# A hybrid encoder layer: a new beginning, and the squares of queries and keys folded onto 64 partitions

## The chip, the cores and the metric

The kernel is one program on one core of one Trainium2 chip. The metric is the device time of an execution in microseconds (us). Three executions of the kernel before took 1318.42, 1318.89 and 1319.12 us. One more was taken with the profiler, and all rows quoted here come from that one. A core has five engines with queues of their own: PE (TensorE, the matmuls), ACT (ScalarE), DVE (VectorE), POOL (GpSimd) and SP (which here only issues DMAs). An instruction waits in the queue of its engine until the semaphores that it names have been reached, and everything behind it on that engine waits with it.

## The reference, cut to what matters

One layer on a sequence of 512 frames with 2048 channels, all in float32:

```python
hn = rmsnorm(x, norm_g)
proj = hn @ w_in                      # q, k, v, gate path of three branches, 4 forget logits, 3 x 2048 merge gates
qa, ka = rmsnorm(q_A, g0), rmsnorm(k_A, g1)      # per head, over its 128 channels
ya = softmax(qa ka^T * scale + c_q - c_k) v_A    # forgetting attention, causal
qb, kb = rmsnorm(q_B, g2), rmsnorm(k_B, g3)
yb = softmax(qb kb^T * scale + rel_bias) v_B     # banded by chunks of 64
yc = stick_breaking(q_C, k_C, v_C)               # no norm of q and k
ys = [ya, yb, yc] * silu(gate path)
merged = sum(sigmoid(gates) * (ys @ w_up))
out = x + merged @ w_out
```

Each branch has 4 heads of 128 channels. So the norm of a query or a key, one sum of 128 squares per frame, is taken 16 times: 4 heads, branches A and B, query and key.

## The kernel before, in words

Everything is transposed: a tile has 128 channels on the partitions and the 512 frames along its rows. A float32 matmul is done with two float32r parts of each operand: the high part is the rounded value, the low part is what is left. `split` makes them, the high part with an ACT copy (L245), the low part with a DVE subtraction (L249). Three products, high by high, high by low and low by high, make one full product.

The kernel is a list of *units*, blocks of weights that are loaded (SP, and POOL where a second block is added in the DMA), split into `wh` and `wl`, and used by the matmuls of L264. The first quad of units computes q, k, v and gate path of the head C0 directly, while x is still arriving. The units after it take pairs of columns with Strassen's seven products, with sums of blocks made on DVE (L631, L637). Attention of the heads is put between the units: C0 to C3, B0 to B3, A0 to A3. Then come the up projections, the merge and the output projection.

The order of work on PE, ACT and DVE is not written out by hand. A planner (`Flow`, L62) runs over generators at build time. Each `yield` names an engine and an estimated cost, or an event or a free buffer to wait for; the planner takes at each step the piece that can start first, and issues it. What comes out is a fixed order on each engine. If a cost in a generator is changed, then pieces around it can change places. POOL and SP are ordered by the program's own order.

The beginning (L291 to L334). `begin_in` is one tile with 128 x 645 floats: the first 512 columns are the channels 0 to 127 of x, and the other 133 are the constants `norm_g` (16), `qk_norm_g` (4), `b_f` (1), `b_gate` (48) and the weights of the forget logits (64). It is SP's first DMA (L294). The first block of weights is ACT's first DMA. POOL sets constants; `onef`, the ones, is its third tile. DVE copies `gqk` into `gq` (L328), scales two columns of it (L330), and copies the forget weights into `w2` (L333), as soon as `begin_in` is there. PE has 16 matmuls of the ones with themselves (L1553, 128x256, bfloat16), whose result nobody reads. Then `prep_x(0)` makes the high part of the first x tile on DVE (L433), `prep` the high part of the first weights on ACT in two halves (L388), and the first matmul of L264 takes both.

The norm of a query or key is `Head.normed`: a multiplication with the norm of x (DVE, L513); the squares (ACT, L912); `split` of the squares (ACT L245 into `sqh`, DVE L249 into `sql`); two matmuls with a matrix of ones that add up over the partitions (L919 for `sqh`, L920 for `sql`, into one PSUM tile); then `rsqrt` with ACT's logarithm and exponential and a step of Newton (L455 to L467); the product with `gq` (L928), and the split into `qkh` and `qkl` that the scores use (L259 to L261). `t2s` counts free tiles of 128x512 floats, `atts` the PSUM tiles for attention.

Of the kernel before, what the change touches and what calls it, by code (L numbers as in the profile page):

```python
# [8 lines left out]
F32 = mybir.dt.float32  # L9
F32R = mybir.dt.float32r  # L10
BF16 = mybir.dt.bfloat16
AF = mybir.ActivationFunctionType
ALU = mybir.AluOpType
AX = mybir.AxisListType

P = 128
S = 512
D = 2048
HD = 128
NH = 4  # L20
W = 512
NB = 3
KT = D // P
QB = S // P
DT = D // P
UK = 8
NQ = 4
HS = S // 2
EPS = 1e-6
NEG = -1e30  # L30
SCALE = HD ** -0.5
# [4 lines left out]
PE, ACT, DVE = 0, 1, 2  # L36
# [26 lines left out]
class Flow:  # L63
# [16 lines left out]
    def give(self, slots, n=1):  # L80
        slots.free += [self.fin] * n

    def spawn(self, gen, slack, ready=None):
        task = Task(gen, slack, self.now if ready is None else ready)
        self.tasks.append(task)
        self.advance(task)
# [62 lines left out]
def mm_us(n, x=1):  # L149
    return x * max(0.115, n / 2400 + 0.0133)  # L150


def act_us(n, x=1):
    return x * (0.075 + 0.00095 * n)


def dve_us(n, x=1):
    return x * (0.1 + 0.00105 * n)
# [3 lines left out]
def hybrid_kernel(  # L162
# [2 lines left out]
    xT: bass.AP,  # L165
    xn: bass.AP,
    begin: bass.AP,
    w_one: bass.AP,
    w_two: bass.AP,
    w_col: bass.AP,  # L170
# [5 lines left out]
    nc = tc.nc  # L176
    PS = bass.MemoryType.PSUM

    cp = ctx.enter_context(tc.tile_pool(name="cp", bufs=1))
# [10 lines left out]
    def nm(s):  # L190
        uid[0] += 1
        return f"{s}_{uid[0]}"

    flow = Flow()
    spawn, set_, give = flow.spawn, flow.set, flow.give
    t2s, atts, raws, xps = Slots(NT, KEPT), Slots(4), Slots(NR), Slots(NX)
    accs = [Slots(2), Slots(1), Slots(1)]

    def t2(s, dt=F32):
        return tp.tile([P, S], dt, tag="t2", name=nm(s))  # L200

    def small(s):
        return sp.tile([P, 1], F32, tag="small", name=nm(s))

    def acc(i=0):

        return pa.tile([P, S], F32, tag=f"acc{i}", name=nm("acc"), bufs=1 if i else 2)

    def att():
        return pt.tile([P, S], F32, tag="att", name=nm("att"))  # L210

    def f(ap):
        return ap.bitcast(F32)

    def blk(i):
        return slice(i * P, (i + 1) * P)

    LH, RH = slice(0, HS), slice(HS, S)

    def two(ap):  # L220

        return ap.rearrange("p (h s) -> p h s", h=2)
# [16 lines left out]
    def pair_of(name, dt=F32R):  # L239
        return t2(name + "h", dt), t2(name + "l", dt)  # L240

    def split(hi, lo, src, n, ev=None, due=(), hi_ev=None):

        yield (ACT, act_us(n), *due)
        nc.scalar.activation(hi, src, AF.Copy)  # L245
        if hi_ev is not None:
            set_(hi_ev)
        yield (DVE, dve_us(n), *due)
        nc.vector.tensor_sub(lo, src, f(hi))  # L249
        if ev is not None:  # L250
            set_(ev)
# [38 lines left out]

    nc.scalar.preload_act_table_set("natural_log_exp_and_others")  # L291
    begin_in = cp.tile([P, begin.shape[1]], F32, name="begin_in")
    x_begin, small_in = begin_in[:, :S], begin_in[:, S:]
    first = [tc.keep_in_program_order(nc.sync.dma_start(begin_in, begin))]  # L294
    gn = small_in[:, 0:KT]
    gqk = small_in[:, KT:KT + 4]
    bfc = small_in[:, KT + 4:KT + 5]
    bg = small_in[:, KT + 5:KT + 5 + NB * DT]
    wf = small_in[:, KT + 5 + NB * DT:].rearrange("p (k h) -> p k h", h=NH)

    epsc = cp.tile([P, 1], F32, name="epsc")
    nc.gpsimd.memset(epsc, EPS)
    nhepsc = cp.tile([P, 1], F32, name="nhepsc")
    nc.gpsimd.memset(nhepsc, -0.5 * EPS)
    tmpc = t2("tmpc")
    onef, zerof, nu_f = tmpc[:, blk(0)], tmpc[:, blk(1)], tmpc[:, blk(2)]
    nc.gpsimd.memset(onef, 1.0)
    nc.gpsimd.memset(zerof, 0.0)
    ones_r = cp.tile([P, P], F32R, name="ones_r")
    nc.vector.tensor_copy(ones_r, onef)  # L310
# [14 lines left out]
    nc.gpsimd.memset(zeroc, 0.0)  # L325

    gq = cp.tile([P, 4], F32, name="gq")
    nc.vector.tensor_copy(gq, gqk)  # L328
    for c in (0, 2):
        nc.vector.tensor_scalar_mul(gq[:, c:c + 1], gqk[:, c:c + 1], SCALE)  # L330

    w2 = cp.tile([P, KT * NH + 32], F32, name="w2")
    nc.vector.tensor_copy(w2[:, :KT * NH].rearrange("p (k h) -> p k h", k=KT), wf)  # L333
    nc.vector.tensor_copy(w2[:, KT * NH:], zerof[:, :32])  # L334
    t2s.free.pop()


# [28 lines left out]
    def raw_tile(shape=(UK, P)):  # L366
        return wp.tile([P] + list(shape), F32, tag="raw", name=nm("raw"), bufs=NR)

    def load_unit(u):
        if isinstance(u, Pair):  # L370
            if u is u.task.units[0]:
                yield from u.task.load()
            return
        for s in u.srcs:
            yield raws, 1
            t = raw_tile(u.shape)
            u.raw = t
            u.there.t = fetch(t, s, flow.ready, 4 * u.shape[0] * P * P // 1024, nc.scalar if u is units[0] else nc.sync).t
# [47 lines left out]
    def prep_x(kt):  # L426

        due = (2.5 + 2.7 * place[kt],)
        yield x_in[kt]
        x, g, h, lo = xraw[kt], gn[:, kt:kt + 1], xs[kt].hi, xs[kt].lo  # L430
        if kt == 0:
            yield (DVE, 0.5, *due)
            nc.vector.tensor_scalar_mul(h, two(x), g)  # L433
        else:
            yield (ACT, act_us(S), *due)
            nc.scalar.activation(h, two(x), AF.Copy, scale=g)
        set_(raw_hi[kt])
        yield (DVE, dve_us(S), *due)
        nc.vector.scalar_tensor_tensor(lo, two(x), g, f(h), op0=ALU.mult, op1=ALU.subtract)
        set_(raw_ev[kt])  # L440

        due = (DUE[0] - 16.0 + place[kt],)
        if kt % 2 == 0:
            yield (DVE, 0.5, *due)
            nc.vector.tensor_scalar_mul(x, x, g)
        else:
            yield (ACT, 0.65, *due)
            nc.scalar.activation(x, x, AF.Copy, scale=g)
        set_(gained[kt])
# [431 lines left out]
    class Head:  # L881
# [23 lines left out]
        def normed(self, r):  # L905
            yield self.event(r)
            c = self.c[r]
            yield from by_norm(c)
            yield t2s, 3
            yield ACT, act_us(S)  # L910
            sq = t2("sq")
            nc.scalar.activation(sq, c, AF.Square)  # L912
            hi, lo = pair_of("sq")
            yield from split(hi, lo, sq, S)
            give(t2s)
            yield atts, 1
            yield PE, mm_us(S, 2)
            ps = att()
            nc.tensor.matmul(ps, ones_r, hi, start=True, stop=False)  # L919
            nc.tensor.matmul(ps, ones_r, lo, start=False, stop=True)  # L920
            give(t2s, 2)
            yield t2s, 4
            rs = t2("rs")
            yield from rsqrt(rs, ps, HD, (t2("rt"), t2("rw"), t2("rv")), S, lambda: give(atts))
            give(t2s, 3)
            i = 2 * self.n + r
            yield DVE, dve_us(S)
            nc.vector.scalar_tensor_tensor(rs, rs, gq[:, i:i + 1], c, op0=ALU.mult, op1=ALU.mult)  # L928
            give(t2s)
            yield t2s, 2  # L930
            self.c[r] = pair_of("qk")
            yield from split(*self.c[r], rs, S, self.event("p", r))
            give(t2s)
# [566 lines left out]
    def loads():  # L1500
        def x(kt):
            if kt == 0:
                xraw[kt], x_in[kt].t = x_begin, landing(0.0, 256)
                return
            yield t2s, 1
            xraw[kt] = t2("x")
            x_in[kt].t = fetch(xraw[kt], xT[kt], 0.0, 256).t

        def n(i):
            yield t2s, 1  # L1510
            t = t2("xn")
            n_in[i].t = fetch(t, xn[i // NQ, i % NQ], 0.0, 256).t
            spawn(square_x(i, t), 10.0)

        todo = list(range(NQ * QB))
        for i, sp in enumerate(spans):

            for kt in [kt for sp in spans[i:i + (2 if i > 2 else 1)] for kt in range(*sp)]:
                if xraw[kt] is None:
                    yield from x(kt)  # L1520
            yield from load_unit(units[i])
            if i >= N_FROM:
                for _ in range(N_PER):
                    if todo:
                        yield from n(todo.pop(0))
        for i in todo:
            yield from n(i)
        for u in units[len(spans):]:
            yield from load_unit(u)
# [21 lines left out]
    warm = onef.bitcast(BF16)  # L1551
    for _ in range(WARM):
        nc.tensor.matmul(first_ps[:, :2 * P], warm[:, :P], warm, start=True, stop=True)  # L1553

    line[:] = 0.8, 1.9
    flow.fin = 3.5
    spawn(loads(), 0.0, 0.0)
    for kt in range(KT):
        spawn(prep_x(kt), 5.0)
    for k in range(UK):  # L1560
        spawn(combos(k), 5.0)
    spawn(stream(), 1e9)
# [4 lines left out]
NT = 20  # L1567
KEPT = 1
AHEAD = 0.4
WARM = 16  # L1570
SPANS = [(0, 1), (1, 2)] + [(k + h, k + h + 2) for k in range(0, UK, 2) for h in (0, UK)][1:]
N_ONE = 2
NX = 28
# [56 lines left out]
```

## Time and profile before

| What | us |
|---|---|
| median of three runs (lowest, highest) | 1318.89 (1318.42, 1319.12) |
| the profiled execution's own time | 1318.54 |
| span of its instructions | 1316.8 |
| busy: PE, DVE, ACT, POOL | 1311.3, 1140.6, 807.2, 95.0 |
| instructions: PE matmuls, DVE, ACT | 7474, 1707, 1280 |
| first matmul of the warm-up, first of L264 | 1.13, 5.31 |

The span runs from the first to the last instruction of the program in the trace; 1.7 us of the execution lie around it. A row of the timeline gives the start, the time from the first start to the last end, the engine and line, what is written and read, and how many instructions were merged into the row; the bracket at the end tells the idle time before it and what ended it. A matmul's duration (0.39 us for 128x512) is longer than the distance to the next one, since matmuls are pipelined; PEld is the load of its weights. The granted TensorE clock of the execution is 1.00 throughout.

### The profile page before, as it was taken

The numbers are of one execution on the slowest core, as the hardware profiler recorded it, in microseconds if no ns is written. First come the engines' busy times: TensorE is split into PE (matmuls) and PEld (weight loads), VectorE is DVE, ScalarE is ACT, GpSimd is POOL, SyncE is SP. The second block draws the span as 40 slices with busy tenths as digits, with TensorE's granted clock in tenths as the row PEclk, the third lists the DMA queues.
The fourth block names the chain that finished last, engine by engine and source line by source line (L and its number), as shares of the span: only waits on it lengthen the run. The fifth ranks groups of instructions, "written<-read, shape, count | busy, mean of one in ns | idle before, by whom it ended". The sixth has DMA issues, their size and how long they took to land.

```text
span 1316.8 us, 20264 instructions
## 1 busy us (share of the span) xinstructions
PE 1311.3 (100%) x7474; PEld 1149.1 (87%) x7474; DVE 1140.6 (87%) x1707; ACT 807.2 (61%) x1280; POOL 95.0 (7%) x120
## 2 busy tenths in 40 slices
PE   9999999999999999999999999999999999999998
PEld 6898888888888888888888888888888888898887
DVE  8999989788898889888898989889899988897786
ACT  8766757575557665666656664666657655454443
POOL 0010100000010100101000000001000000000100
PEclk9999999999999999999999999999999999999999
DMA  9777767767776776766767767776769765668883
GB/s 339 213 204 198 183 192 185 200 186 192 201 199 187 188 200 179 219 181 189 202 179 216 188 184 199 205 185 185 195 179 280 248 219 168 206 172 253 242 248 100
DMA packets 89651, 266.24 MB, mean 202 GB/s; under 512 B 10560, under 2 KB 12608, under 8 KB 89552
## 3 DMA queue, kind: packets, MB, share of 16 engines
q1 hardware_dynamic: 70400, 203.86, 45.5%
q0 software_dynamic: 15552, 56.63, 25.4%
q10 hardware_dynamic: 3600, 4.46, 0.9%
q8 instruction: 59, 0.97, 0.3%
q14 instruction: 40, 0.33, 0.1%
HBM read 245.21 MB, written 19.70 MB: 201 GB/s over the span
## 4 chain that ended last, share of the span: by engine, by line
PE 99%; DVE 1%; DMA 0%; ACT 0%; issue 0%; ACTq 0%
PE acc L264 85%; PE att L264 8%; PE att L1022 1%; PE att L260 1%; PE att L1136 1%; PE att L261 1%; PE att L1137 1%; PE att L259 1%; PE att L1135 1%; PE att L1087 0%; PE att L1237 0%; PE att L919 0%; PE att L920 0%; DMA begin_in<-in_begin 0%; DVE m L249 0%; DVE wl L249 0%
## 5 line engine op out<-in xcount | busy, mean ns | idle before, releaser
L249 DVE TENSOR_TENSOR wl<-raw,wh 128x1024 fp32r<-128x1024 f32 (+2 forms) x418 | 499.0, 1198 | 122.2 <-ACT wh L245 121.5
L245 ACT ACTIVATE wh<-raw 128x1024 fp32r<-128x1024 f32 (+2 forms) x418 | 433.7, 1039 | 162.9 <-PE acc L264 89.9
L264 PE MATMUL acc<-x,wh 128*128 128x512 f32 (+1 forms) x1568 | 396.7, 388 | 0.7 <-DVE gq L330 0.7
L264 PEld LDWEIGHTS acc<-x,wh 128*128 128x128 f32 x1568 | 283.7, 188 | 56.1 <-issue 2.2
L264 PE MATMUL acc<-t,wh 128*128 128x512 f32 (+1 forms) x1128 | 280.3, 388 | 0.0
L264 PEld LDWEIGHTS acc<-t,wh 128*128 128x128 f32 x1128 | 200.4, 189 | 34.8
L264 PEld LDWEIGHTS acc<-x,wl 128*128 128x128 f32 x1504 | 205.9, 190 | 16.5 <-issue 0.8
L264 PE MATMUL acc<-x,wl 128*128 128x256 f32 (+1 forms) x1504 | 216.5, 285 | 0.0
L264 PE MATMUL acc<-t,wl 128*128 128x256 f32 x1104 | 156.5, 283 | 0.0
L264 PEld LDWEIGHTS acc<-t,wl 128*128 128x128 f32 x1104 | 144.7, 191 | 2.1
L282 POOL DMA_DIRECT2D raw<-in_w_col x92 | 79.7, 866 | 916.3 <-DMA raw<-in_w_col 449.3
L264 PE MATMUL acc<-m,wh 128*128 128x512 f32 (+1 forms) x512 | 109.7, 364 | 0.3 <-DVE m L249 0.3
L264 PEld LDWEIGHTS acc<-m,wh 128*128 128x128 f32 x512 | 86.3, 189 | 13.9 <-DVE m L249 0.5
L825 ACT ACTIVATE c<-acc 128x256 f32<-128x256 f32 x51 | 19.6, 384 | 90.8 <-PE acc L264 85.3
L771 ACT ACTIVATE u<-acc 128x512 f32<-128x512 f32 x52 | 31.1, 598 | 65.6 <-PE acc L264 60.3
L631 DVE TENSOR_TENSOR raw<-raw,raw 128x1024 f32<-128x1024 f32 x54 | 65.8, 1219 | 0.3
L637 DVE TENSOR_TENSOR raw<-raw,raw 128x1024 f32<-128x1024 f32 x54 | 65.8, 1218 | 0.3
L264 PE MATMUL att<-y,wh 128*128 128x512 f32 x256 | 65.8, 389 | 0.0
L792 ACT ACTIVATE u<-acc 128x512 f32<-128x512 f32 x51 | 30.3, 595 | 55.1 <-PE acc L264 54.2
L264 PEld LDWEIGHTS acc<-m,wl 128*128 128x128 f32 x448 | 58.3, 191 | 2.4
L264 PE MATMUL acc<-m,wl 128*128 128x256 f32 x448 | 59.8, 283 | 0.0
L264 PEld LDWEIGHTS att<-y,wh 128*128 128x128 f32 x256 | 48.0, 188 | 10.0
(202 smaller groups left out, 1388.6 us busy)
## 6 DMA issues: line engine op xcount, KB each, us to landing
raw<-in_w_col SPq DMA_DIRECT2D x230, 512.0 KB, 4.4
raw<-in_w_col POOLq DMA_DIRECT2D x92, 512.0 KB, 6.4
raw<-in_w_out SPq DMA_DIRECT2D x40, 512.0 KB, 4.3
gl<-c SPq DMA_DIRECT2D x48, 256.0 KB, 3.1
raw<-in_w_up SPq DMA_DIRECT2D x32, 384.0 KB, 3.1
sg<-gl SPq DMA_DIRECT2D x48, 256.0 KB, 4.4
raw<-in_w_out POOLq DMA_DIRECT2D x16, 512.0 KB, 7.3
xn<-in_xn SPq DMA_DIRECT2D x16, 256.0 KB, 3.6
```

The lines of the kernel that those rows point to most:

```text
L245: nc.scalar.activation(hi, src, AF.Copy)
L249: nc.vector.tensor_sub(lo, src, f(hi))
L259: nc.tensor.matmul(ps, lh, rh, start=start, stop=False, skip_group_check=more)
L260: nc.tensor.matmul(ps, lh, rl, start=False, stop=False, skip_group_check=more)
L261: nc.tensor.matmul(ps, ll, rh, start=False, stop=stop, skip_group_check=more)
L264: nc.tensor.matmul(ps, w, x, start=start, stop=stop, skip_group_check=more)
L282: nc.gpsimd.dma_start(to, src, accum_op=ALU.add)
L631: nc.vector.tensor_add(w[1], w[1], w[5])
L637: nc.vector.tensor_add(w[2], w[2], w[1])
L771: nc.scalar.activation(self.u, ps, AF.Copy)
L792: nc.scalar.activation(self.s, ps, AF.Copy)
L825: nc.scalar.activation(c, ps[:, RH], AF.Copy, scale=-1.0)
```

## The change

There are two parts.

In the beginning, `begin_in` keeps only the first x tile and `norm_g` (128 x 528 floats). The other constants become a tensor of their own, `consts`, with 117 columns, that goes to `small_in` by a DMA on ACT's queue, issued right behind the DMA of the first weights. The copies into `gq` and `w2` become a piece of the plan, `small_parts`, that is not to start before 9 us of planned time. POOL sets `onef` first. The number of warm-up matmuls goes from 16 to 19.

In `normed`, the squares are taken in two ACT instructions of 64 partitions each: partitions 0 to 63 into `sa`, partitions 64 to 127 into the partitions 0 to 63 of `sb`. DVE adds them (64x512). The high part of that sum goes to partitions 0 to 63 of one tile, the low part to partitions 64 to 127 of the same tile. One matmul with the ones over 128 partitions then adds up high and low parts at once, where there were two. This is done for all 16 queries and keys.

```diff
+HP = P // 2
...
     begin_in = cp.tile([P, begin.shape[1]], F32, name="begin_in")
-    x_begin, small_in = begin_in[:, :S], begin_in[:, S:]
+    small_in = cp.tile([P, consts.shape[1]], F32, name="small_in")
+    x_begin, gn = begin_in[:, :S], begin_in[:, S:]
     first = [tc.keep_in_program_order(nc.sync.dma_start(begin_in, begin))]
-    gn = small_in[:, 0:KT]
...
+    tmpc = t2("tmpc")
+    onef, zerof, nu_f = tmpc[:, blk(0)], tmpc[:, blk(1)], tmpc[:, blk(2)]
+    nc.gpsimd.memset(onef, 1.0)
     epsc = cp.tile([P, 1], F32, name="epsc")
...
     gq = cp.tile([P, 4], F32, name="gq")
-    nc.vector.tensor_copy(gq, gqk)
-    for c in (0, 2):
-        nc.vector.tensor_scalar_mul(gq[:, c:c + 1], gqk[:, c:c + 1], SCALE)
-
     w2 = cp.tile([P, KT * NH + 32], F32, name="w2")
-    nc.vector.tensor_copy(w2[:, :KT * NH].rearrange("p (k h) -> p k h", k=KT), wf)
     nc.vector.tensor_copy(w2[:, KT * NH:], zerof[:, :32])
+
+    def small_parts():
+        yield DVE, 0.8
+        nc.vector.tensor_copy(w2[:, :KT * NH].rearrange("p (k h) -> p k h", k=KT), wf)
+        nc.vector.tensor_copy(gq, gqk)
+        for c in (0, 2):
+            nc.vector.tensor_scalar_mul(gq[:, c:c + 1], gqk[:, c:c + 1], SCALE)
...
             yield t2s, 3
-            yield ACT, act_us(S)
-            sq = t2("sq")
-            nc.scalar.activation(sq, c, AF.Square)
-            hi, lo = pair_of("sq")
-            yield from split(hi, lo, sq, S)
+            yield ACT, act_us(S, 2)
+            sa, sb = t2("sa"), t2("sb")
+            nc.scalar.activation(sa[:HP], c[:HP], AF.Square)
+            nc.scalar.activation(sb[:HP], c[HP:], AF.Square)
+            yield DVE, dve_us(S)
+            nc.vector.tensor_add(sa[:HP], sa[:HP], sb[:HP])
+            give(t2s)
+            parts = t2("sq", F32R)
+            yield from split(parts[:HP], parts[HP:], sa[:HP], S)
             give(t2s)
             yield atts, 1
-            yield PE, mm_us(S, 2)
+            yield PE, mm_us(S)
             ps = att()
-            nc.tensor.matmul(ps, ones_r, hi, start=True, stop=False)
-            nc.tensor.matmul(ps, ones_r, lo, start=False, stop=True)
-            give(t2s, 2)
+            nc.tensor.matmul(ps, ones_r, parts, start=True, stop=True)
+            give(t2s)
...
             yield from load_unit(units[i])
+            if i == 0:
+                nc.scalar.dma_start(small_in, consts)
...
+    spawn(small_parts(), 2.0, 9.0)
...
-WARM = 16
+WARM = 19
...
-        "begin": np.concatenate([xT[0]] + consts, axis=1),
+        "begin": np.concatenate([xT[0], consts[0]], axis=1),
+        "consts": np.concatenate(consts[1:], axis=1),
```

In the order that the planner makes of it, the first of a head's two matmuls with the ones (the key's) stands 12 matmuls of L264 later than its pair did, and the second (the query's) 10 later. ACT takes the four squares in a row where it took two, then a `wh`, then the two high parts; DVE takes the two additions in a row, then a `wl`, then the two low parts. The four instructions of `small_parts` follow DVE's first eight instructions of the x tiles and weights. In the head A3, the last one, the transposes of the probabilities (L1022 before) stand 22 matmuls of L264 earlier than they did, and the products with v 16 earlier. From the up projections on, PE's order is the same.

More of the change, by code (lines that the diff above doesn't have):

```diff
@@ L167, in hybrid_kernel @@
     begin: bass.AP,
+    consts: bass.AP,
     w_one: bass.AP,
@@ L292, in hybrid_kernel @@
     begin_in = cp.tile([P, begin.shape[1]], F32, name="begin_in")
-    x_begin, small_in = begin_in[:, :S], begin_in[:, S:]
+    small_in = cp.tile([P, consts.shape[1]], F32, name="small_in")
+    x_begin, gn = begin_in[:, :S], begin_in[:, S:]
     first = [tc.keep_in_program_order(nc.sync.dma_start(begin_in, begin))]
-    gn = small_in[:, 0:KT]
[L296 to L299, printed above, removed]
+    gqk = small_in[:, 0:4]
+    bfc = small_in[:, 4:5]
+    bg = small_in[:, 5:5 + NB * DT]
+    wf = small_in[:, 5 + NB * DT:].rearrange("p (k h) -> p k h", h=NH)
+    tmpc = t2("tmpc")
+    onef, zerof, nu_f = tmpc[:, blk(0)], tmpc[:, blk(1)], tmpc[:, blk(2)]
+    nc.gpsimd.memset(onef, 1.0)
     epsc = cp.tile([P, 1], F32, name="epsc")
@@ L304, in hybrid_kernel @@
     nc.gpsimd.memset(nhepsc, -0.5 * EPS)
-    tmpc = t2("tmpc")
-    onef, zerof, nu_f = tmpc[:, blk(0)], tmpc[:, blk(1)], tmpc[:, blk(2)]
-    nc.gpsimd.memset(onef, 1.0)
     nc.gpsimd.memset(zerof, 0.0)
```

## The prediction

> **What bounds the kernel now.** I read the page first (busy time and the chain that ended last), then PE's waits, then the table by stretches, and last the timeline at the three places that the change touches.
>
> ```profile
> span 1316.8 us, 20264 instructions
> PE 1311.3 (100%) x7474; PEld 1149.1 (87%) x7474; DVE 1140.6 (87%) x1707; ACT 807.2 (61%) x1280; POOL 95.0 (7%) x120
> ```
>
> ```profile
> PE att L1553 <- POOL tmpc L307: 1.1, 1, 1.1
> PE acc L264 <- DVE gq L330: 0.7, 1, 0.7
> PE acc L264 <- DVE m L249: 0.3, 1, 0.3
> ```
>
> PE is busy 1311.3 of 1316.8 us, and these three lines are all its waits: two before its first useful matmul, 0.3 us late in the output projection. The rest of the 5.5 us is the end after the last matmul. A matmul taken out of the packed stretch is therefore worth its whole spacing, as long as no wait appears in its place.
>
> ```profile
> 358.00:445.00 87.00, 87.00 (x503) 76.72 (x502) 74.87 (x111) 54.46 (x85) 6.92 (x8) 1.00 0.72 196
> 867.00:951.00 84.00, 84.00 (x490) 74.36 (x489) 75.48 (x113) 52.03 (x83) 6.92 (x8) 1.00 0.71 193
> 951.00:1030.00 79.00, 79.00 (x457) 69.80 (x456) 72.62 (x116) 57.14 (x93) 4.32 (x5) 1.00 0.78 231
> ```
>
> By stretches (columns: length, PE, PEld, DVE, ACT and POOL busy, granted clock, DMA share, GB/s) the first and the last head with a norm of q and k take 87 and 84 us with PE full, DVE at 86 to 90% and ACT at 62%. The stretch after them has DVE at 92%.
>
> **The change, part by part.** *The matmuls removed.* Timeline around the first head's norm:
>
> ```profile
> 354.69 1.14 ACT L912 ACTIVATE sq<-c 128x512 f32<-128x512 f32 x2
> 355.73 0.62 ACT L245 ACTIVATE sqh<-sq 128x512 fp32r<-128x512 f32 x1
> 356.25 1.05 ACT L245 ACTIVATE wh<-raw 128x1024 fp32r<-128x1024 f32 x1
> 356.76 0.42 DVE L711 TENSOR_TENSOR c<-u 128x256 f32<-128x256 f32 x1
> 357.11 0.69 DVE L249 TENSOR_TENSOR sql<-sq,sqh 128x512 fp32r<-128x512 f32 x1
> 357.20 0.62 ACT L245 ACTIVATE sqh<-sq 128x512 fp32r<-128x512 f32 x1
> 357.71 1.22 DVE L249 TENSOR_TENSOR wl<-raw,wh 128x1024 fp32r<-128x1024 f32 x1
> 358.42 0.39 PE L919 MATMUL att<-sqh,ones_r 128*128 128x512 f32 x1
> 358.66 0.39 PE L920 MATMUL att<-sql,ones_r 128*128 128x512 f32 x1
> 358.85 0.68 DVE L249 TENSOR_TENSOR sql<-sq,sqh 128x512 fp32r<-128x512 f32 x1
> 358.89 0.40 PE L264 MATMUL acc<-t,wh 128*128 128x512 f32 x1
> 360.28 0.39 PE L919 MATMUL att<-sqh,ones_r 128*128 128x512 f32 x1
> 360.51 0.39 PE L920 MATMUL att<-sql,ones_r 128*128 128x512 f32 x1
> 360.74 0.86 PE L264 MATMUL acc<-x,wh 128*128 128x512 f32 x3
> 361.24 1.23 DVE L249 TENSOR_TENSOR wl<-raw,wh 128x1024 fp32r<-128x1024 f32 x1 [1.71 <-ACT wh L245]
> 361.44 0.63 PE L264 MATMUL acc<-x,wl 128*128 128x256 f32 x4
> ```
>
> Two matmuls take 358.89 - 358.42 = 0.47 and 360.74 - 360.28 = 0.46 us, so one is worth 0.2325. One of two goes, 16 times: 16 x 0.2325 = **3.72 us** off PE.
>
> *What is added beside it.* Each norm gets one ACT square and one DVE addition more, all on 64 partitions. No row shows such an instruction with 512 columns on 64 partitions. Nearest are those of 128x512 (ACT 0.62, with 0.52 to the next one; DVE 0.69, with 0.60 to the next) and, with half the elements, DVE's 128x256 at 356.76 (0.42). I take the 128x512 prices, since a partition has the same 512 elements to go through; 0.42 is the lower end, and twice the 128x512 price the upper (a rival). That is at most 16 x 0.52 = 8 us on ACT and 16 x 0.60 = 10 us on DVE over 600 us, beside PE. The cover is idle time such as the 1.71 us before DVE's 361.24.
>
> *Does the norm come too late?* Before, the key's pair needed `sql`, ready at 357.80, and took it at 358.66: 0.86 us to spare. Now, by the same rows in the changed order: four squares from 354.69, 0.52 apart, the last over at 356.87; `wh` to 357.8; the two high parts to 358.34 and 358.86. DVE adds from 357.11 to 358.40, does its `wl` to 359.5, and the low parts until 360.14 (key) and 360.74 (query). PE reaches the key's matmul 12 matmuls later than 358.42: nine with 512 columns (0.23 apart) and three with 256 (0.12, from the row of four at 361.44), at 360.85, and the query's 0.23 + 4 x 0.12 later, at 361.56. To spare: 0.71 and 0.82 us. So no wait, cost nothing; if the cover is gone, PE pays what the chain is late beyond 0.71 us, once a head, 8 times. Logarithm, exponential and scores follow some 30 us later in the units and have more room. The seven other heads have this same order.
>
> *The last head.* Here the plan moved more: the transposes of A3 stand 22 matmuls earlier, so at the end of the row 999.50 below, near 1000.35.
>
> ```profile
> 998.52 0.40 ACT L1005 ACTIVATE p<-p,mx 128x128 f32<-128x128 f32 x1 [0.52 <-DVE mx L1001]
> 998.92 0.49 ACT L1011 ACTIVATE p<-p,sm 128x256 f32<-128x256 f32 x1
> 999.32 1.04 ACT L245 ACTIVATE wh<-raw 128x1024 fp32r<-128x1024 f32 x1
> 1003.74 0.39 ACT L1011 ACTIVATE p<-p,sm 128x128 f32<-128x128 f32 x1
> 999.50 1.12 PE L264 MATMUL acc<-t,wl 128*128 128x256 f32 x8
> 1004.72 1.25 PE L1022 MATMUL att<-identf,p 128*128 128x128 f32 x10
> ```
>
> ACT now does the exponential (to 998.92), a `wh` (to 999.9), and both scalings of `p` behind it (to 1000.65). That is 0.3 us after PE gets there. Bounds: 0 (an earlier exponential) to 1.0 us (a DVE operation of 1.22 in front of the reciprocal). I take **+0.3**.
>
> *The beginning.* Rows of PE, DVE and ACT, and one of 63 us:
>
> ```profile
> 4.50 0.17 DVE L328 COPY gq<-begin_in 128x4 f32<-128x4 f32 x1 [1.93 <-DMA begin_in<-in_begin]
> 4.68 0.48 DVE L433 TENSOR_SCALAR x<-begin_in 128x512 fp32r<-128x512 f32 x1
> 4.69 0.72 ACT L388 ACTIVATE wh<-raw 128x256 fp32r<-128x256 f32 x2 [2.61 <-DMA raw<-in_w_one]
> 1.13 3.48 PE L1553 MATMUL att<-tmpc 128*128 128x256 bf16 x16 [1.13 <-POOL tmpc L307]
> 5.31 0.70 PE L264 MATMUL acc<-x,wh 128*128 128x512 f32 x2 [0.70 <-DVE gq L330]
> 14.61 0.62 PE L1237 MATMUL att<-begin_in,w 128*32 128x512 f32 x1
> 62.35 1.06 ACT L245 ACTIVATE wh<-raw 128x1024 fp32r<-128x1024 f32 x1 [0.29 <-DVE raw L637]
> 63.47 0.39 PE L264 MATMUL acc<-x,wh 128*128 128x256 f32 x1
> ```
>
> Without the two copies x begins at 4.50 instead of 4.68, and a begin that is 18% smaller (528 of 645 columns) lands up to 0.3 us sooner; but the weights' high part still starts at 4.69. The first matmul moves from 5.31 to between 5.0 and 5.25. The 19 matmuls, by 3.48 / 16 = 0.22 each, end near 5.2 and hold nobody up. What is gained is mostly given back at 63.47: there `wh` is over at 63.41, 0.06 before PE, and waits for DVE, which has the same work as before (the copies only come later). So the start is worth 0 to 0.3 us; I take **-0.1**. The new DMA is issued on ACT's queue behind the first weights, while ACT waits anyway (2.61 us). `small_parts` waits on DVE with the later x tiles queued behind; it is wanted by PE at 14.61, and its bytes were in `begin_in` before. Cost 0; up to 1 us if it lands late. The warm-up starts perhaps 0.06 us sooner; nothing hangs on it.
>
> *Sum.* -3.72 + 0.3 - 0.1 = -3.5 us. The profiled execution took 1318.54, its counterpart comes to 1315.0. That execution lies 0.35 under the median of 1318.89, so the forecast is **1315.4**.
>
> **The rivals.** *A. The folded chain is late (slower).* If instructions that read 64 partitions and write the other 64 take twice the time of the 128x512 rows, the squares end at 359.05, the low parts at 362.8 and 364.0, and PE waits 2.0 + 0.5 us in every head: 8 x 2.5 - 3.5 = +16, 1335 us. It decides where the chain is 0.71 + 2 x 0.2325 = 1.18 us later than worked out: then PE's waits eat what the two matmuls gave. For it: DVE is at 86 to 92%. Against: 0.71 us to spare, and idle time right behind.
> *B. One DVE operation of 1.22 us slips in front of the low parts in each head.* 8 x (1.22 - 0.71) = 4.1 us back: 1319.5, no real change. For it: `wl` stands between additions and low parts. Against: that one is counted already.
> *C. A matmul removed is worth less than its spacing*, because its neighbours close up only as far as the weight loads let them. At the spacing of the 256-column rows, 0.12, it gives 1.9 us: 1317.2. Against it stand the equal spacings of 0.23 and 0.24 on both sides of L919 and L920. [...]
> *D. The start gets worse*: `consts` lands late, or takes from the x tiles what PE needs: +1, 1316.4. Against: 10 us from issue to use. [...]
>
> **How the numbers follow.** Forecast 0.78, A 0.05, B 0.06, C 0.05, D 0.06. The forecast alone spans 1314.1 (start 0.3, last head 0, 0.4 for a favourable execution) to 1316.4. Up to C it reaches 1317.2; A and B lie outside. I give 1314.0 to 1317.2. A measurement tells 0.2% (2.6 us) from no change, so faster means under 1316.25: 0.78 of the forecast less a bit at its upper end, plus half of D, makes 0.80. B, C and the rest of D are the same, 0.14; A and worse slips are slower, 0.06.
>
> **What would show it.** Right: 7461 matmuls (7474 - 16 + 3), one 0.39 matmul per norm at a spacing of 0.23, no PE wait on `sq` and none on the scores; DVE busy some 10 us more and ACT 8; the first matmul of L264 at 5.0 to 5.25; at most one PE wait of about 0.3 us near 996 us, on `p`; a span near 1313.3. Wrong: PE waits on `sq` or `qkl` in each head (A, B), a missing wait but less than 3 us gained (C), or waits before 30 us (D).

## The result, and the profile after

| What (us) | before | after |
|---|---|---|
| median of seven executions | 1318.89 | 1315.04 |
| lowest, highest | 1318.41, 1320.61 | 1314.02, 1315.27 |
| the profiled execution, its span | 1318.54, 1316.8 | 1315.27, 1313.6 |

The ratio is 0.9968, with a 95% interval of 0.9958 to 0.9978: 3.9 us or 0.3% faster. The forecast was 1315.4. One of the seven executions before took 1320.61; the experiments show that such executions are a group of their own, with a cause in the beginning.

The busy time of the changed kernel, and all the waits of its PE (what waited, for what: us in total, times, longest):

```profile
span 1313.6 us, 20260 instructions
PE 1308.4 (100%) x7461; PEld 1147.1 (87%) x7461; DVE 1153.4 (88%) x1723; ACT 816.9 (62%) x1296; POOL 94.8 (7%) x120
```

```profile
PE att L1563 <- POOL nhepsc L309: 1.1, 1, 1.1
PE acc L266 <- ACT s L797: 0.4, 1, 0.4
PE acc L266 <- DVE m L251: 0.3, 1, 0.3
```

There are 13 matmuls fewer (16 removed, 3 more in the warm-up). ACT is busy 9.7 us more and DVE 12.8 us more, and PE is still full. PE waits nowhere for a `sq`. One wait is new, 0.4 us for `s` of L797.

The first head's norm in the timeline of the changed kernel, the counterpart of the rows from 354.69 on in the prediction (rows of other work are left out):

```profile
354.76 0.62 ACT L917 ACTIVATE sa<-c 64x512 f32<-64x512 f32 x1
355.39 0.63 ACT L918 ACTIVATE sb<-c 64x512 f32<-64x512 f32 x1
356.05 0.63 ACT L917 ACTIVATE sa<-c 64x512 f32<-64x512 f32 x1
356.70 0.63 ACT L918 ACTIVATE sb<-c 64x512 f32<-64x512 f32 x1
357.18 1.28 DVE L920 TENSOR_TENSOR sa<-sa,sb 64x512 f32<-64x512 f32 x2
357.36 1.06 ACT L247 ACTIVATE wh<-raw 128x1024 fp32r<-128x1024 f32 x1
358.32 1.14 ACT L247 ACTIVATE sq<-sa 64x512 fp32r<-64x512 f32 x2
358.45 1.23 DVE L251 TENSOR_TENSOR wl<-raw,wh 128x1024 fp32r<-128x1024 f32 x1
359.71 1.29 DVE L251 TENSOR_TENSOR sq<-sa,sq 64x512 fp32r<-64x512 f32 x2
360.53 0.51 PE L266 MATMUL acc<-x,wl 128*128 128x256 f32 x3
360.88 0.40 PE L928 MATMUL att<-sq,ones_r 128*128 128x512 f32 x1
361.11 0.63 PE L266 MATMUL acc<-x,wl 128*128 128x256 f32 x4
361.58 0.39 PE L928 MATMUL att<-sq,ones_r 128*128 128x512 f32 x1
```

One matmul per norm, 0.23 us ahead of the next one. The key's low part is over in the middle of DVE's last row, near 360.40, and PE takes it at 360.88: it is 0.48 us early. The query's, over at 361.00, is 0.58 us early.

### The profile page after: what moved, and what is told of

Read it like the earlier page. It is cut to its first block, busy times and chain, and to the rows that moved or that the text cites. A ratio compares the mean times of both kernels' runs of the same rounds, so it can differ in the third digit from the quotient of the medians.

```text
span 1313.6 us, 20260 instructions
## 1 busy us (share of the span) xinstructions
PE 1308.4 (100%) x7461; PEld 1147.1 (87%) x7461; DVE 1153.4 (88%) x1723; ACT 816.9 (62%) x1296; POOL 94.8 (7%) x120
## 4 chain that ended last, share of the span: by engine, by line
PE 98%; DMA 1%; DVE 1%; ACT 0%; issue 0%; POOL 0%; ACTq 0%; DVEq 0%; POOLq 0%
PE acc L266 84%; PE att L266 8%; PE att L1030 1%; PE att L262 1%; PE att L263 1%; PE att L261 1%; PE att L1144 1%; PE att L1145 1%; PE att L1143 0%; DMA gl<-c 0%; PE att L1095 0%; PE att L1563 0%; PE att L1245 0%; PE att L928 0%; DMA raw<-in_w_out 0%
## 5 line engine op out<-in xcount | busy, mean ns | idle before, releaser
L797 ACT ACTIVATE u<-acc 128x512 f32<-128x512 f32 x51 | 30.3, 594 | 77.8 <-PE acc L266 76.1
L776 ACT ACTIVATE u<-acc 128x512 f32<-128x512 f32 x52 | 31.2, 599 | 67.4 <-PE acc L266 64.2
```

Of the source, the lines that this page charges most:

```text
L776: nc.scalar.activation(self.u, ps, AF.Copy)
L797: nc.scalar.activation(self.s, ps, AF.Copy)
```

## The experiments

The time of an execution has three parts that the change can touch, and the traces give each. Starts are in us from the beginning of the span; "heads" runs from the second group of four transpositions of L1087 (L1095 after), near 161.5, to the first matmul of the up projections, and holds all 16 norms.

| execution | first useful matmul | first matmul of the forget logits | length of "heads" |
|---|---|---|---|
| before | 5.31 | 14.61 | 863.75 |
| after | 5.02 | 14.82 | 860.47 |
| the changed kernel, once more | 5.37 | 15.06 | 859.68 |
| fold alone, 16 warm-ups | 5.64 | 16.75 | 860.37 |
| beginning alone | 5.48 | 14.79 | 863.74 |
| before with 19 warm-ups | 5.45 | 14.74 | 863.75 |
| changed with 16 warm-ups | 5.88 | 15.17 | 859.56 |
| fold with two matmuls | 5.53 | 14.83 | 863.34 |
| high part alone | 5.33 | 14.65 | 859.75 |

**The two parts, each alone.** The fold is put into the kernel before, whose beginning stays (16 warm-up matmuls; the order of the matmuls behind them is that of the changed kernel):

```diff
-            yield ACT, act_us(S)
-            sq = t2("sq")
...
+            nc.scalar.activation(sa[:HP], c[:HP], AF.Square)
+            nc.scalar.activation(sb[:HP], c[HP:], AF.Square)
...
+            nc.tensor.matmul(ps, ones_r, parts, start=True, stop=True)
```

> The kernel before with the folded squares alone (beginning unchanged, 16 warm-up matmuls). Theory: the whole gain is the 16 matmuls less (16 x 0.2325 = 3.72 us) minus the one wait of 0.4 us in the last head; the start is worth nothing: 1315.4 us, between 1315.0 and 1315.9, PE idle less than 1 us beyond the start. Rival (the start carries part of the gain): 1316 or more.

Measured: 1316.61, between 1314.94 and 1317.67 (9 executions); ratio 0.9969 (0.9959 to 0.9979). The executions fall into two groups with nothing between: four from 1314.94 to 1315.53, five from 1316.61 to 1317.67. The kernel before does the same beside it: 10 of 25 from 1318.48 to 1319.02, 15 from 1320.12 to 1320.94. The median lies in the rival's range, because more than half of the executions are of the upper group. Group against group, the fold alone gives the whole gain; but the forecast knew of one group only.

And the new beginning without the fold (the edit is shown against the changed kernel, whose fold it takes back; the order of the matmuls behind the warm-up is that of the kernel before):

```diff
-            nc.tensor.matmul(ps, ones_r, parts, start=True, stop=True)
+            nc.tensor.matmul(ps, ones_r, hi, start=True, stop=False)
+            nc.tensor.matmul(ps, ones_r, lo, start=False, stop=True)
```

> The kernel before with the new beginning alone (two matmuls with the ones as before, 128-partition squares). Theory: no change, 1318.9 us, between 1318.4 and 1319.3; the first matmul of L266 starts at about 5.0 instead of 5.3, and what is won is lost again before 66 us or to the slow start of PE's clock. Rival: the start carries 0.5 us or more, 1318.3 or less.

Measured: 1318.59, 1318.41 to 1319.08 (11 executions); ratio 0.9991 (0.9982 to 1.0). There is one group, and it is the lower one of the kernel before. So the beginning makes the executions of the lower group no shorter by a measurable amount; what it does is that the upper group is gone.

The profiled execution of the fold alone took 1317.18, one of the upper group and the only profile of it. PE's timeline at its start:

```profile
1.13 3.60 PE L1557 MATMUL att<-tmpc 128*128 128x256 bf16 x16 [1.13 <-POOL tmpc L308]
5.64 1.19 PE L265 MATMUL acc<-x,wh 128*128 128x512 f32 x2 [0.91 <-DVE gq L331]
6.63 1.05 PE L265 MATMUL att<-x,wh 128*128 128x512 f32 x2
7.48 1.05 PE L265 MATMUL acc<-x,wh 128*128 128x512 f32 x2
8.34 1.05 PE L265 MATMUL att<-x,wh 128*128 128x512 f32 x2
9.19 0.80 PE L265 MATMUL acc<-x,wl 128*128 128x512 f32 x2
```

PE stands idle for 0.91 us behind the warm-up. Then pairs of matmuls follow each other every 0.85 us, 0.427 for one, until 9.2 us. In the changed kernel:

```profile
1.06 4.24 PE L1563 MATMUL att<-tmpc 128*128 128x256 bf16 x19 [1.06 <-POOL nhepsc L309]
...
5.02 1.22 PE L266 MATMUL acc<-x,wh 128*128 128x512 f32 x2
6.04 0.67 PE L266 MATMUL att<-x,wh 128*128 128x512 f32 x2
6.54 0.62 PE L266 MATMUL acc<-x,wh 128*128 128x512 f32 x2
```

PE has no gap; the first pair is slow, and from 6.04 on a pair takes about 0.5 us or less. The forget logits come at 14.82 there and at 16.75 with the fold alone: 1.93 us, about the distance of the groups (1.6 to 1.9 by their medians).

**What in the beginning does it?** The number of warm-ups alone was changed, up in the kernel before and down in the changed one.

```diff
-WARM = 16
+WARM = 19
```

> The kernel before with 19 warm-up matmuls instead of 16, nothing else. Theory (the warm-up closes the gap of PE in front of the first data, so that PE's clock goes up before the first useful matmuls or within two of them, in every execution): all executions between 1318.4 and 1319.3, none near 1320.5. Rival (the smaller first DMA and the moved copies do it): executions at 1318.5 and at 1320.5 as with 16.

Measured: 1318.76, 1318.54 to 1319.31 (11 executions), one group; the kernel before beside it had 9 of 21 from 1318.51 to 1318.93 and 12 from 1320.38 to 1321.09. Ratio 0.9991 (0.9982 to 1.0).

```diff
-WARM = 19
+WARM = 16
```

> The changed kernel with 16 warm-up matmuls, nothing else. Theory: executions fall into two groups again, near 1315 and near 1316.7, and the spread is over 1.5 us. Rival: all near 1315, spread under 1.3 us.

Measured: 1316.33; two executions of 1314.69, three from 1316.33 to 1317.0; ratio 0.9966 (0.9954 to 0.9979). The upper group goes with three more warm-ups and comes back without them, whatever else the beginning holds. The rest of the new beginning (constants moved, `begin_in` smaller) is worth 1318.76 - 1318.59 = 0.2 us by these two medians, which are from two chips; that cannot be told from nothing.

How do 19 warm-ups do it? PE's timeline of the kernel before with 19, in an execution in which the matmuls reached their full speed (0.23 us from one of 128x512 to the next) early:

```profile
1.13 3.71 PE L1553 MATMUL att<-tmpc 128*128 128x256 bf16 x19 [1.13 <-POOL tmpc L307]
5.45 0.70 PE L264 MATMUL acc<-x,wh 128*128 128x512 f32 x2 [0.61 <-DVE gq L330]
6.00 0.62 PE L264 MATMUL att<-x,wh 128*128 128x512 f32 x2
```

The same 19 matmuls take 3.71 us here and 4.24 in the changed kernel, since their last ones follow each other faster here. Behind them is a gap of 0.61 us, and it does no harm: the first pair takes 0.55 to the next. Nor does a gap of 1.35 us in the profiled execution of the changed kernel with 16 (1314.69, of the lower group), where the first pair takes 0.56. Where full speed is late, the 19 warm-ups themselves are longer (4.23 and 4.24 us) and reach at least to within 0.2 us of the first data. The beginning alone has such a short gap, and the first pair behind it takes 0.57:

```profile
1.06 4.23 PE L1560 MATMUL att<-tmpc 128*128 128x256 bf16 x19 [1.06 <-POOL nhepsc L309]
5.48 0.73 PE L266 MATMUL acc<-x,wh 128*128 128x512 f32 x2 [0.18 <-ACT wh L393]
6.05 0.62 PE L266 MATMUL att<-x,wh 128*128 128x512 f32 x2
```

So in these profiles a gap does harm at most where full speed is late and the gap is long (0.91 us in the fold alone). That 19 warm-ups remove the upper group is shown; that they do it by closing the gap is argued from these rows.

**The matmul's worth, and the cost of the folding.** In the changed kernel the one matmul is issued twice into the same tile, and the mean is taken over twice as many:

```diff
-            nc.tensor.matmul(ps, ones_r, parts, start=True, stop=True)
+            nc.tensor.matmul(ps, ones_r, parts, start=True, stop=False)
+            nc.tensor.matmul(ps, ones_r, parts, start=False, stop=True)
```

> The changed kernel with the fold, but the one matmul with the ones is issued twice into the same sum, and the norm divides by twice the number of channels, so that the result is the same. Theory: 16 matmuls are back, 1315.04 + 3.7 = 1318.7 us, within 0.5. Rival (a matmul is worth less than its spacing, 0.12 us each): 1317.0.

Measured: 1318.09, 1317.82 to 1318.86 (10 executions); ratio 0.9988 (0.9979 to 0.9997). That is 3.05 us above the changed kernel's median, and 0.1 below the range expected: the changed kernel's own profile has a wait for `s` (below) that this run has not. The stretch tells it more closely: "heads" takes 863.34, against 859.68 and 859.56 in the profiled executions of the changed kernel, once more and with 16 warm-ups, which have no wait for `s` either: 3.66 and 3.78 us for 16 matmuls, 0.23 each. The planner was told of the cost and moved some pieces by a few matmuls; but the second matmul itself starts 0.234 us behind the first, in the mean of the 16.

Then the other half: no fold and no stacking, a square over 128 partitions and its high part alone in one matmul.

```diff
-            nc.scalar.activation(sa[:HP], c[:HP], AF.Square)
-            nc.scalar.activation(sb[:HP], c[HP:], AF.Square)
...
+            nc.scalar.activation(sq, c, AF.Square)
+            hi = t2("sqh", F32R)
+            nc.scalar.activation(hi, sq, AF.Copy)
...
+            nc.tensor.matmul(ps, ones_r, hi, start=True, stop=True)
```

> The changed kernel with 128-partition squares and one matmul of their high parts; the low parts of the squares are left out, with their DVE subtraction, and so are the fold and its additions. Theory: the same 16 matmuls are gone, so as the changed kernel, 1315.0 us, within 0.5; that the DVE and ACT work of the fold is gone changes nothing. Rival (the fold's longer chain costs PE something in each head): 1314.3 or less.

Measured: 1314.42, 1314.38 to 1314.51 (4 executions), a little below the range expected; ratio 0.9958 (0.9944 to 0.9972). "Heads" takes 859.75, as long as with the fold (859.68), though this plan puts the matmuls with the ones 15 to 17 other matmuls earlier. So the squares, additions and low parts of the fold cost PE nothing. The profiled execution (1314.38) is 0.44 us shorter than that of the changed kernel once more (1314.82), and 0.41 of it is there at the forget logits already (14.65 and 15.06).

**How far is the chain from being late?** One more DVE instruction of 64x512, whose result nobody reads, behind each addition:

```diff
             nc.vector.tensor_add(sa[:HP], sa[:HP], sb[:HP])
+            nc.vector.tensor_mul(sb[:HP], sa[:HP], sa[:HP])
```

> The changed kernel with one more DVE multiplication of 64x512 behind each addition of the folded squares (its result is not used), of which the plan knows nothing, so that all orders stay. It makes the low parts 2 x 0.60 = 1.2 us later in each head; they have 0.48 us to spare (key). Theory: PE waits 0.7 us on sq in each of 8 heads, 1315.0 + 5.8 = 1320.8 us, between 1319.5 and 1322. Rival (idle time of DVE takes it up): 1315.0 to 1315.6, no PE wait.

Measured: 1322.78, 1322.39 to 1323.61 (8 executions); ratio 1.0023 (1.0013 to 1.0033). PE's waits and its timeline:

```profile
PE att L929 <- DVE sq L251: 6.1, 8, 0.8
```

```profile
360.33 0.51 PE L266 MATMUL acc<-x,wl 128*128 128x256 f32 x3
361.60 0.50 PE L929 MATMUL att<-sq,ones_r 128*128 128x512 f32 x1 [0.77 <-DVE sq L251]
```

This is 0.8 above the upper end of what was expected. PE now waits once in each of the eight heads. From the row of three before it to the matmul it is 1.27 us, where the changed kernel had 360.88 - 360.53 = 0.35: 0.92 per head, of which the profile calls 0.77 idle (a matmul's modelled end lies behind the start of its successor: the one at 360.88 in the changed kernel is 0.40 us long, and the next starts 0.23 behind it). The matmul behind the wait then takes 0.33 to the next, where the changed kernel has 0.23: 0.10 more. Per head 1.02, and 8 x 1.02 = 8.2: "heads" takes 867.87, 8.19 more than the changed kernel without the wait for `s` (859.68). The median went up by 7.7. Two instructions of 0.68 us in a chain with 0.48 to spare turn the gain of 3.9 us into a loss of 3.9.

**Why did the squares take longer than forecast?** `sb` is read from the lower half too, so that no square goes from one half of the partitions to the other (the squares of the upper half are left out):

```diff
-            nc.scalar.activation(sb[:HP], c[HP:], AF.Square)
+            nc.scalar.activation(sb[:HP], c[:HP], AF.Square)
```

> The changed kernel with both squares taken from partitions 0 to 63 (the squares of the channels 64 to 127 are left out, those of 0 to 63 are counted twice). Theory: ACT's distance from one square to the next falls from 0.65 to 0.52 us, since it is the move from the upper to the lower partitions that costs the overlap; the low parts have about 0.4 us more to spare; the time stays within 0.5 of 1315.0. Rival: the distance stays at 0.65, since it belongs to squares of 64 partitions.

One execution, 1314.12. ACT's timeline:

```profile
354.45 0.62 ACT L917 ACTIVATE sa<-c 64x512 f32<-64x512 f32 x1
354.97 0.62 ACT L918 ACTIVATE sb<-c 64x512 f32<-64x512 f32 x1
355.49 0.61 ACT L917 ACTIVATE sa<-c 64x512 f32<-64x512 f32 x1
356.01 0.62 ACT L918 ACTIVATE sb<-c 64x512 f32<-64x512 f32 x1
```

Each instruction takes 0.62 us as before, but they start 0.52 apart, where the squares of both halves start 0.63 to 0.66 apart. So the squares of the upper half cost overlap with the neighbours. Whether it is their move to the lower half, or that squares of lower and upper half take turns, this run cannot tell, since it takes both away. "Heads" takes 859.55 us, no less than without it.

**The new wait in the last head.** The changed kernel was run again as it is.

> The changed kernel as it is, beside the kernel before on the same chip, in five rounds. Theory: all executions between 1314.0 and 1315.6 in one group, while the kernel before falls into two groups near 1318.7 and 1320.6; the gain is 3.7 us against the one and 5.6 against the other. Rival: the changed kernel has two groups as well.

Measured: 1315.35, 1314.18 to 1315.73 (7 executions), one group; the kernel before beside it had 8 of 11 from 1318.58 to 1319.04 and 3 from 1320.37 to 1320.56. Ratio 0.997 (0.9959 to 0.9981). Its profiled execution (1314.82) has no wait for `s`; that of the first profile (1315.27) has. ACT's timeline in that first one, and PE's:

```profile
1008.14 0.60 ACT L780 ACTIVATE v<-acc 128x512 f32<-128x512 f32 x1 [3.16 <-DMA gl<-c]
1008.64 1.05 ACT L247 ACTIVATE wh<-raw 128x1024 fp32r<-128x1024 f32 x1
1009.59 3.23 ACT L247 ACTIVATE y<-yr 128x512 fp32r<-128x512 f32 x6
1012.71 0.58 ACT L797 ACTIVATE s<-acc 128x512 f32<-128x512 f32 x1
```

```profile
1013.34 0.86 PE L266 MATMUL acc<-t,wl 128*128 128x256 f32 x5 [0.43 <-ACT s L797]
```

The copy of L780 waits 3.16 us for a buffer that a store of gates still reads. Behind it ACT has a `wh` and six splits of `y`, and only then the `s` that frees a PSUM tile for PE. In the other execution L780 begins at 1007.60, held by PE and not by the store, `s` is over at 1012.75, and PE comes at 1012.98. Matched matmul by matmul from the last norm on, the execution with the wait is 0.70 us behind at this place and 0.78 at the first up projection.

Other runs with the same order of matmuls bear this out. With the fold alone that copy (L776 there) waits 3.06 us for the store, and PE waits 0.33 for `s`. With 16 warm-ups and with the squares of one half it waits 2.10 and 1.85 us for the store, and PE does not wait for `s`.

Two ways to take the wait away: one more buffer of `t2s`, and one offset of the plan that puts the products with v later among the matmuls.

```diff
-NT = 20
+NT = 21
```

> The changed kernel with 21 free tiles of 128x512 instead of 20. Theory (the one new wait, 0.4 us on L797 in the last head, comes from ACT's 3.2 us wait for a tile that a store still reads): ACT's wait at L780 goes, PE's wait on s goes, 1314.6 us, between 1314.1 and 1315.0. Rival (the six splits of y in front of L797 hold it back): the wait on s stays, 1315.0.

Measured: 1313.9, 1313.87 to 1314.2 (4 executions); ratio 0.9961 (0.9947 to 0.9974). ACT's timeline:

```profile
1005.54 0.60 ACT L780 ACTIVATE v<-acc 128x512 f32<-128x512 f32 x1 [0.56 <-PE acc L266]
1006.98 3.23 ACT L247 ACTIVATE y<-yr 128x512 fp32r<-128x512 f32 x6
1010.24 0.60 ACT L797 ACTIVATE s<-acc 128x512 f32<-128x512 f32 x1
```

L780 no longer waits for the store, the six splits still stand in front of `s`, and `s` is over at 1010.84, 2.45 us earlier. So the splits alone do not make `s` late; with the buffer free the wait is gone. This is the fastest version here, 0.2 below the range expected, but the plan is another one throughout: the output projection alone is 157.06 instead of 157.61 us long, and that has nothing to do with the wait.

```diff
-OFF = dict(..., av1=3, ...)
+OFF = dict(..., av1=4, ...)
```

> The changed kernel with the last head's product with v one unit later (av1=4). Theory: the plan gets another order around L797; the wait for the tile that a store still reads may go or stay, 1314.5 to 1315.2; no other wait appears. Rival: the merge behind the last head then waits for y, 1315.5 or more.

Measured: 1314.31, 1313.96 to 1314.97 (4 executions), 0.2 below the range expected; ratio 0.9964 (0.995 to 0.9977). It has no wait for `s` either; "heads" takes 859.59 us. Since the unaltered order has executions without the wait too, a profile of this one does not show that the offset is what takes it away.

## Why the prediction was right

*The matmuls.* 16 x 0.2325 = 3.72 us stands: 3.66 and 3.78 were measured by putting them back, and 0.234 us from start to start. Rival C (a matmul is worth less than its spacing), with 1.9 us for the 16, is out.

*The added work* is a little more than the bounds taken, ACT 9.7 against 8 us and DVE 12.8 against 10: the price of a 128x512 instruction was the right one for 64 partitions (0.62 and 0.68 us in duration), but per norm ACT is busy 0.61 us more instead of 0.52 and DVE 0.80 instead of 0.60, since overlap with neighbours is lost (ACT's squares start about 0.65 us apart instead of 0.52). It is hidden, as forecast.

*The chain of the norm.* PE's side was right to 0.03 us (360.88 and 361.58 against 360.85 and 361.56). The room was mis-sized: 0.48 and 0.58 us instead of 0.71 and 0.82. DVE lost it: the additions ended at 358.46 instead of 358.40, and from `wl` to the low part it is 359.71 - 358.45 = 1.26 us, where the rows before had 358.85 - 357.71 = 1.14. ACT was later too, with the last square over at 357.33 instead of 356.87, but the additions hid that, and in the run with both squares on one half nothing was gained. The conclusion, no wait, held with a third less room than stated. The other conclusion, that beyond this room PE pays in each head, was right too: 1.02 us a head, and the sign of the change turns. So rival A named the real danger and had the wrong multiple: such instructions took the time of 128x512 ones (0.62 to 0.63 us on ACT, 0.68 on DVE), plus about a tenth of a microsecond of lost overlap at some borders. Rival B (one more DVE operation) did not come.

*The last head, +0.3.* Here the step failed. PE does not wait for the probabilities:

```profile
994.07 0.81 ACT L1019 ACTIVATE p<-p,sm 128x256 f32<-128x256 f32 x2 [0.19 <-DVE sm L1017]
996.23 1.25 PE L1030 MATMUL att<-identf,p 128*128 128x128 f32 x10
```

Both scalings are over at 994.88, 1.35 us before PE comes. I had only moved PE's part in the old rows; ACT's had moved forward as well, with both scalings begun at 994.07. In place of that wait there is the one for `s`, 17 us later, of 0.70 us in the stretch, and only in some executions. Its cause, a buffer still read by a store, was in none of the steps.

And the new order is itself shorter: with the matmuls put back "heads" is 863.34 against 863.75, 0.41 us that no step had. It comes off at the norms. Two rows of PE on both sides of the first head's, from the kernel before, the fold with two matmuls and the changed kernel:

```profile
356.80 1.78 PE L264 MATMUL acc<-t,wh 128*128 128x512 f32 x7
362.38 1.12 PE L264 MATMUL acc<-t,wl 128*128 128x256 f32 x8
...
356.88 2.00 PE L266 MATMUL acc<-t,wh 128*128 128x512 f32 x8
362.41 1.12 PE L266 MATMUL acc<-t,wl 128*128 128x256 f32 x8
...
356.87 2.00 PE L266 MATMUL acc<-t,wh 128*128 128x512 f32 x8
361.93 1.12 PE L266 MATMUL acc<-t,wl 128*128 128x256 f32 x8
```

With the same other matmuls in between, the distance is 5.58 us before, 5.53 with both matmuls in the new place, and 5.06 with one. By the starts of single matmuls the two steps are 0.060 and 0.467 us, in each of the eight heads: 8 x 0.467 = 3.74 for the matmuls, and 8 x 0.060 = 0.48 for their new place (the fold with two matmuls loses 0.07 of that elsewhere). The new place is among matmuls of 256 columns, the old one was among such of 512; why it is cheaper no run shows. Behind the last norm 0.93 is lost, 0.78 of it with the wait for `s`. So "heads" changes by -3.74 - 0.48 + 0.93 = -3.29; measured 860.47 - 863.75 = -3.28. That it came out near the forecast's -3.72 + 0.3 = -3.42 is luck: the gain of 0.48 and the loss of 0.93, neither of them forecast, stand in place of the 0.3 of a wait that did not come.

*The beginning, -0.1.* Right for the executions that were in the forecast's view: the beginning alone is 1318.59 against the lower group's 1318.41 to 1319.12, and what the logits gain or lose is partly given back by 161.5 us (14.61 and 14.82 become 161.49 and 161.56). The first useful matmul came at 5.02, inside the range of 5.0 to 5.25; but the other profiles with the new beginning and 19 warm-ups have it anywhere from 5.20 to 5.53, and the kernel before has it at 5.31. Rival D (`consts` late) is out: PE waits for nothing of it. But the sentence that the 19 warm-ups "hold nobody up" took them for harmless and asked nothing about what they are for. They are worth about 1.8 us in the executions of the upper group, and these were more than half on two of the chips used (15 of 25 and 12 of 21; 3 of 11 on a third). The three executions that the forecast had were all of the lower group, as was the profile. So the gain is 3.7 us against the lower group and about 5.5 against the upper one; the figure of 3.9 depends on the share of each among the seven.

## What to carry to other kernels

Price a matmul in a packed stream by its distance to the next one (0.23 us here, where its row says 0.39), and a chain that feeds it by how early it is: 0.5 us of room was enough for no cost at all, and 1.3 us more work on DVE turned 3.9 us of gain into 3.9 of loss. Let warm-up matmuls run until the first data is there, and look at all executions of a kernel rather than at three: two groups 1.8 us apart became one with three more warm-up matmuls. When a planner has moved a stretch, rows of the old trace on one engine do not say when the others will get there.

## What the runs showed of the hardware

The slow matmuls at the start were not expected. The warm-ups of 128x256 are 0.213 us apart, and the first useful ones of 128x512 are 0.427 apart in the fold alone, nearly twice the 0.12 and 0.23 of later rows; the profile's granted clock says 1.00 all the while, as in this row of the table by stretches of the fold alone (columns as in the prediction):

```profile
5.00:9.40 4.40, 3.76 (x9) 3.03 (x10) 4.33 (x11) 3.99 (x8) 0.00 (x0) 1.00 1.05 404
```

Nine matmuls start in the 3.76 us in which PE is busy here; at 0.23 there is room for 16. So where the expectations speak of PE's clock, what was measured is the distance between matmuls. When full speed comes differs from execution to execution: in the profiles shown it is before 5 us (before with 19 warm-ups, which take 3.71 us in all), a little after 6.0 (the changed kernel) and near 9.5 (fold alone, behind a gap of 0.91 us, 4.73 to 5.64). What sets it no run shows; that the gap is the reason is argued from these times and from the runs with 16 and 19 warm-ups.

An instruction over 64 partitions took as long here as one over 128 (512 columns: 0.62 to 0.63 us for either on ACT, 0.68 for an addition over 64 and 0.68 to 0.69 for a low part over either on DVE). What is lost is overlap with neighbours. On DVE the first low part, which reads the lower half of the partitions and writes the upper, starts 1.26 us behind its `wl` instead of 1.14. The second, which goes from the lower to the upper half as well, follows it as closely as before: the two take 1.29 us together. So on DVE not every move between halves loses overlap; in these rows it was lost between the `wl` over 128 partitions and the first low part. On ACT the squares of lower and upper half take turns and start about 0.65 us apart instead of 0.52; there no run tells the change from the move.
